# Query product by sevens beside twenty units, with one of its sums made by an accumulating transfer, and another order of the output product

## The chip, the cores and the metric

The kernel runs on one core of one Trainium2 chip. TensorE (PE) multiplies matrices and accumulates in PSUM, VectorE (DVE) adds and multiplies elementwise, ScalarE (ACT) applies functions and casts, GpSimd (POOL) does small odd work and can issue transfers, SyncE (SP) issues transfers only. Each of these engines takes its own instructions in order. The metric is the device time of one execution in microseconds (us); the time given for a kernel is the median of several runs.

## The reference

Two layers run over 256 tokens of width 2048, in float32. Cut to what matters:

```python
for l in range(2):
    h = rms_norm(x, norm1_g[l])
    z = h @ w_in[l]                      # 2048 x 3584: u, v | q | k, v
    z_sgu = gelu(z[..., :2048])          # u and v of the spatial gate, 1024 columns each
    out_a = chunked_sgu(z_sgu, ...)      # u * (causal w_s @ rms_norm(v) + b_s), chunks of 128
    out_b = swa_sink_attention(q, k, v)  # 16 query heads, 4 key heads, window 128, a sink
    mixed = concat(rms_norm(out_a), rms_norm(out_b))
    x = x + mixed @ w_out[l]             # 2048 x 2048
    h2 = rms_norm(x, norm2_g[l])
    x = x + (silu(h2 @ w_gate[l]) * (h2 @ w_up[l])) @ w_down[l]   # inner width 5632
return x
```

## The kernel before

**Products in three passes.** A float32 product is made of three passes in a shorter format: each operand is split into a high part and the rest, and `mm3` (L140 to L142) multiplies high by high, high by rest (`wl`), rest by high. Weights are split as they come: `raw_load` (L97) brings 512 KB, 256 rows by 512 columns, into one of seven buffers `raw`; `split2` has ACT cast it to `wh` (L106, five buffers) and DVE subtract to get `wl` (L107, four buffers). A standard `unit` is one such load and 12 matmuls of 128x512, for the 256 tokens.

**Products by seven.** `seven` computes a 256-row by 2-block product from seven products instead of eight. A weight is seen as blocks b11, b12, b21, b22; the activations have four sums of their blocks, `ext`, made ahead by `extend` (sums `e` on DVE at L265, L268, L271; cast of `ext` on ACT at L275 and subtraction on DVE at L276). For each of four row groups i it loads b11, b12, b22 and runs five `s_unit`s of 6 matmuls: b11, then b11+b12 (sum on DVE, L315), then t2 = b11+b12+b22 (L316), then b22, then b12+b22 (L319). After its use t2 is made into one more sum by a transfer that POOL issues and that adds b21 from memory onto it (L321). After the four groups come four units of b21 and four of the kept t2, between them the closing sums of the banks (`m0` to `m4`, L332 and L336). A product by seven takes 30 steps. Its banks are five PSUM tiles `m`; the standard product beside it takes two others, `dacc`.

**Order.** The program is written as one stream of units. `tick` counts a clock, one for a unit and a half for an `s_unit`; `later(delay, fn)` puts a piece of work at a later count of this clock. The position in the stream decides where a piece stands in the queue of each engine. A scheduler then orders each engine's queue by it.

**Layer 0, its first part.** Eight units of the k and v block (block 4 of `w_in`), then eight each of blocks 2 and 3 (v of the spatial gate). After the first eight (`Q_FROM`), the query product by seven runs beside the remaining `Q_UNITS` = 16 units. The extensions of the activations come at clock `EXT_AT` + half the pair's number after the pair was loaded; x is loaded by rows, at 8 + 3i, and squared for its norm by ACT (L220). `begin` (clock 21) makes the inverse norm; `inv_rms` has DVE make `ms` (L194) and POOL raise it to the power -1/2 (`ir`, L196). `head_inv` squares v, sums per head (`hs`, L238), and after a gap of 2.5 units scales (`scaled` of `v_gate`, L606 and L607). `kv_norm` and `q_norm` do the same for k (L426) and q (L462).

**Attention, gates and the output product.** Six attention units (`attend`, placed by `UNIT_AT`) and four transposes (`END_AT`) run beside the two u blocks of `w_in` and the output product. `spatial` multiplies v by the gate's weights (`ps_g`, L592) into PSUM tiles that `small_ps` takes in turn from three pools; `u_gated` applies the Gelu to u (L620) and transposes it. The output product has a part a (from the spatial gate, four units per column block) and a part b (from attention); `part` adds each to x (L713). `norm_block` transposes the finished column block of x, and makes the activations and their sums for the feed-forward part (`combine`, L282 and L283, and `extend`).

**Feed-forward.** Ten of eleven inner blocks run by seven, 300 steps, beside 104 standard units for the eleventh block and the product with `w_down`. `FF_FIRST` = 3 of the standard units come before the first step; the rest are spread evenly over the steps. In layer 1 the query product by seven runs at the end of layer 0's feed-forward part and beside the first units of layer 1.

Of the kernel before, what the change touches and what calls it, by code (L numbers as in the profile page):

```python
# [20 lines left out]
P = 128  # L21
# [35 lines left out]
SPATIAL_AT = (((6, 9), (6, 9)), ((6, 9), (7, 10)))  # L57
U_AT = (((2, 5), (2, 3)), ((3, 7), (2, 3)))
END_AT = (((23, 27), (31, 33)), ((22, 27), (31, 33)))
FF_FIRST = 3  # L60
EXT_AT = 5
GATE_LOAD = ((14, 23), (5, 15))

# [12 lines left out]
def trunk(ctx, tc, x, xt, w_in, w_q, w_out, w_gate, w_up, w_down, sgu_w, sgu_g, consts,  # L76
# [105 lines left out]
    tab = cp.tile([P, 16], F32, tag="tab", name="tab")  # L182
    nc.scalar.copy(tab, mhalf)
    ident = cp.tile([P, P], F32, tag="ident", name="ident")
# [76 lines left out]

    def extend(g, pool, tag):
# [8 lines left out]
        nc.vector.scalar_tensor_tensor(  # L271
            e[:, 3, :], e[:, 2, :], -1.0, q[:, 2, :], ALU.mult, ALU.subtract
        )
        x = pool.tile([P, 2, 4, P], F32R, tag=tag, name="ext", bufs=8)
        nc.scalar.copy(x[:, 0], e)  # L275
        nc.vector.tensor_tensor(x[:, 1], e, f(x[:, 0]), ALU.subtract)  # L276
        return x

    def combine(ps, lay, col, ext):
        g = gained(ps, lay, col)  # L280
        pair = tp.tile([P, 2, 2, SEQ], F32R, tag="hT", name="hT")
        nc.scalar.copy(pair[:, 0], g)  # L282
        nc.vector.tensor_tensor(pair[:, 1], g, f(pair[:, 0]), ALU.subtract)  # L283
        ext.append(extend(g, ap, "big"))
        return pair

    def seven(src, pairs, ext, out, end=lambda sg: None):
        bank = [pa.tile([P, NB], F32, tag="acc", name=f"m{i}") for i in range(5)]
# [18 lines left out]
        for i in range(4):  # L307
            b11 = raw_load(src(0, 0, i))
            b12 = raw_load(src(0, 1, i))
            b22 = raw_load(src(1, 1, i))  # L310
            t2 = ap.tile([P, 2, NB], F32, tag="spt", name="t2", bufs=4)
            first, last = i == 0, i == 3
            s_unit(b11, 0, i, a_op(0, 0), first, last)
            yield
            nc.vector.tensor_tensor(b11, b11, b12, ALU.add)  # L315
            nc.vector.tensor_tensor(t2, b11, b22, ALU.add)  # L316
            s_unit(b11, 1, i, e_op(1), first, last)
            yield
            nc.vector.tensor_tensor(b12, b12, b22, ALU.add)  # L319
# [35 lines left out]
    def q_product(lay, pairs, ext):  # L355
        q = {"k": 0}
        q["steps"] = seven(
            lambda r, c, i: w_q[lay, c, i, r], pairs, ext, lambda *a: q["out"](*a)
        )
        return q  # L360
# [11 lines left out]
    def first_pair(p, pairs=pairs1, ext=ext1):  # L372
        if p % 2 == 0:
            xrs[0] = ap.tile([P, 4, SEQ], F32, tag="big", name="xr", bufs=8)
        xr = xrs[0][:, 2 * (p % 2) : 2 * (p % 2) + 2, :]
        nc.sync.dma_start(xr, xt[:, 2 * p : 2 * p + 2, :])
        pairs.append(split_gain(xr, 0, C_G1 + 2 * p, "hT"))
        later(EXT_AT + 0.5 * p, lambda: ext.append(extend(gained(xr, 0, C_G1 + 2 * p), tp, "aT")))

# [10 lines left out]
    for i in range(2 * NTOK):  # L390
        later(8 + 3 * i, lambda i=i: load_x(i // 2, i % 2))
    now_q = q_product(0, pairs1, ext1)

    for lay in range(L):
        layer = {}

        def begin(lay=lay, layer=layer, ss1=ss1):
            layer["rstd1"] = finish_rms(ss1, D)
            nsink = small([P, NH], "nsink")
            nc.vector.tensor_scalar(nsink, cst[:, lay, C_SK : C_SK + NH], -1.0, None, ALU.mult)  # L400
            layer["nsink"] = nsink
            nr = small([P, NTOK], "nr")
            layer["nrstd1"] = [nr[:, t : t + 1] for t in range(NTOK)]
            for t in range(NTOK):
                nc.vector.tensor_scalar(
                    layer["nrstd1"][t], layer["rstd1"][t], -1.0, None, ALU.mult
                )

# [3 lines left out]
        def kv_norm(acc, lay=lay, layer=layer, zkv=zkv, kT=kT):  # L412
# [167 lines left out]
        def v_gate(b, acc, lay=lay, layer=layer, gate=gate):  # L580
# [27 lines left out]

            head_inv([v[:, t] for t in range(NTOK)], 8, scaled, 2.5)
            for half in range(2):  # L610
# [55 lines left out]

        later(1 if lay > 0 else 21, begin)
        beside = (pd, "dacc")
# [11 lines left out]
        for i, (gp, t, i0, n) in enumerate(units):  # L680
            at = UNIT_AT[i]
# [34 lines left out]

        early = [part("a", n) for n in range(2)]
        for p in early:
            next(p)
            next(p)  # L720
        for p in early:
            run(p)
        for n in range(2, ND):
            run(part("a", n))
# [281 lines left out]
```

## Time and profile before

| | us |
|---|---|
| median of three runs | 1935.85 (1935.37 to 1936.84) |
| the profiled execution, its own time | 1935.13 |
| its span in the trace | 1933.3 |
| PE busy in the span | 1916.8 |
| DVE busy | 1737.3 |
| ACT busy | 1344.0 |
| POOL busy | 133.5 |

All durations below are of the profiled execution, which lies 0.7 us under the median; some 1.8 us of its time lie outside the span. Matmuls are pipelined: a record of 0.39 us starts 0.227 us after the one before it, so PE's time is read from starts, and a row whose bracket says `[0.73 <-ACT wh L106]` had PE standing 0.73 us until that instruction of ACT ended. The granted clock of TensorE is given for each window: 1.00 is full speed.

### The profile page before, as it was taken

Reading aid. Unit: us, or ns where it says so; the run is one execution under the profiler, and the core shown is the slowest. Engines: PE = TensorE matmul, PEld = TensorE weight load, DVE = VectorE, ACT = ScalarE, POOL = GpSimd, SP = SyncE. Lnnn points to the kernel's source line nnn. Section 1 sums busy time; section 2 is a strip of 40 time slices with the busy share of each in tenths; the row PEclk is TensorE's granted clock in tenths of the full one; section 3 lists DMA queues with packets and bytes.
Section 4 is the critical chain, followed back from the end, with each engine's and each line's share of the span. In section 5 each row is a group of like instructions: output and inputs, shape, how many; then the busy total and the mean of one; then the engine's idle time right before and its main releaser. Section 6 shows DMA issues by size and latency. Waiting matters only on the chain.

```text
span 1933.3 us, 25197 instructions
## 1 busy us (share of the span) xinstructions
PE 1916.8 (99%) x8788; PEld 1570.8 (81%) x8788; DVE 1737.3 (90%) x1870; ACT 1344.0 (70%) x1798; POOL 133.5 (7%) x128
## 2 busy tenths in 40 slices
PE   9999999999999999999999999999999999999999
PEld 6788887888888888888888888878888888888887
DVE  8977679999999999999797766899999999999993
ACT  8667566677676776767777574766776677767774
POOL 0220000000000000000001300000000000000000
PEclk9999999999999999999999999999999999999999
DMA  8865356768677776678567544477678677867773
GB/s 313 250 215 180 133 180 202 227 224 278 209 243 238 247 250 222 230 254 268 189 210 265 176 145 165 163 233 222 227 243 266 223 226 240 275 215 241 240 258 123
DMA packets 120368, 430.62 MB, mean 223 GB/s; under 512 B 13360, under 2 KB 14000, under 8 KB 120240
## 3 DMA queue, kind: packets, MB, share of 16 engines
q1 hardware_dynamic: 105264, 375.52, 52.4%
q0 software_dynamic: 14400, 52.44, 14.8%
q8 instruction: 69, 1.13, 0.2%
q10 hardware_dynamic: 576, 1.05, 0.2%
q14 instruction: 59, 0.48, 0.1%
HBM read 426.85 MB, written 2.10 MB: 222 GB/s over the span
## 4 chain that ended last, share of the span: by engine, by line
PE 93%; DVE 4%; issue 1%; ACT 1%; POOL 1%; DMA 0%; SPq 0%; DVEq 0%; ACTq 0%
PE m L141 14%; PE m L142 14%; PE m L140 14%; PE dacc L140 10%; PE dacc L141 10%; PE dacc L142 10%; PE acc L140 6%; PE acc L141 6%; PE acc L142 6%; DVE wl L107 2%; PE ps_v L545 1%; PE ps_f L213 1%; PE ps_s L496 1%; POOL ir L196 1%; PE ps_t L213 1%
## 5 line engine op out<-in xcount | busy, mean ns | idle before, releaser
L106 ACT CAST wh<-raw 128x1024 fp32r<-128x1024 f32 (+1 forms) x794 | 812.8, 1049 | 391.0 <-DVE raw L315 153.6
L107 DVE TENSOR_TENSOR wl<-raw,wh 128x1024 fp32r<-128x1024 f32 (+1 forms) x794 | 945.3, 1219 | 93.0 <-PE acc L141 33.3
L141 PE MATMUL m<-wl,ext 128*128 128x512 f32 x704 | 277.5, 394 | 5.7 <-DVE wl L107 5.7
L140 PE MATMUL m<-wh,ext 128*128 128x512 f32 x704 | 278.2, 396 | 3.3 <-ACT wh L106 3.0
L142 PE MATMUL m<-wh,ext 128*128 128x512 f32 x704 | 275.4, 391 | 0.0
L140 PE MATMUL dacc<-wh,aT 128*128 128x512 f32 x624 | 243.6, 392 | 0.0
L141 PE MATMUL dacc<-wl,aT 128*128 128x512 f32 x624 | 243.1, 390 | 0.0
L142 PE MATMUL dacc<-wh,aT 128*128 128x512 f32 x624 | 243.0, 390 | 0.0
L107 DVE TENSOR_TENSOR wl<-t,wh 128x1024 fp32r<-128x1024 f32 x176 | 212.2, 1219 | 9.0 <-PE dacc L141 3.5
L106 ACT CAST wh<-t 128x1024 fp32r<-128x1024 f32 x176 | 184.3, 1051 | 46.6 <-DVE t L316 21.6
L140 PE MATMUL m<-wh,hT 128*128 128x512 f32 x528 | 205.9, 390 | 0.0
L141 PE MATMUL m<-wl,hT 128*128 128x512 f32 x528 | 205.5, 389 | 0.0
L142 PE MATMUL m<-wh,hT 128*128 128x512 f32 x528 | 205.5, 389 | 0.0
L141 PEld LDWEIGHTS m<-wl,ext 128*128 128x128 f32 x704 | 132.5, 188 | 38.0 <-DVE wl L107 11.3
L140 PEld LDWEIGHTS m<-wh,ext 128*128 128x128 f32 x704 | 132.4, 188 | 35.3 <-ACT wh L106 8.3
L142 PEld LDWEIGHTS m<-wh,ext 128*128 128x128 f32 x704 | 132.5, 188 | 26.7
L321 POOL DMA_DIRECT2D t<-in_w_gate_dram x80 | 69.7, 871 | 1148.0 <-DVE wl L107 1032.7
L140 PEld LDWEIGHTS dacc<-wh,aT 128*128 128x128 f32 x624 | 117.2, 188 | 25.2 <-ACT dacc L820 1.0
L141 PEld LDWEIGHTS dacc<-wl,aT 128*128 128x128 f32 x624 | 117.2, 188 | 24.4
L142 PEld LDWEIGHTS dacc<-wh,aT 128*128 128x128 f32 x624 | 117.1, 188 | 24.3
L140 PE MATMUL acc<-wh,aT 128*128 128x512 f32 x336 | 134.7, 401 | 0.0
L142 PE MATMUL acc<-wh,aT 128*128 128x512 f32 x336 | 131.4, 391 | 0.0
(148 smaller groups left out, 2796.4 us busy)
## 6 DMA issues: line engine op xcount, KB each, us to landing
raw<-in_w_gate_dram SPq DMA_DIRECT2D x176, 512.0 KB, 5.6
raw<-in_w_up_dram SPq DMA_DIRECT2D x176, 512.0 KB, 5.5
raw<-in_w_down_dram SPq DMA_DIRECT2D x176, 512.0 KB, 4.9
t<-in_w_gate_dram POOLq DMA_DIRECT2D x80, 512.0 KB, 5.8
raw<-in_w_in_dram SPq DMA_DIRECT2D x76, 512.0 KB, 4.8
raw<-in_w_out_dram SPq DMA_DIRECT2D x64, 512.0 KB, 3.2
raw<-in_w_q_dram SPq DMA_DIRECT2D x32, 512.0 KB, 5.0
t<-in_w_q_dram POOLq DMA_DIRECT2D x8, 512.0 KB, 7.2
```

The source lines that it names most:

```text
L106: nc.scalar.copy(wh[:, j : j + step, :], src)
L107: nc.vector.tensor_tensor(wl[:, j : j + step, :], src, f(wh[:, j : j + step, :]), ALU.subtract)
L140: nc.tensor.matmul(acc, ah, wh, start=first, stop=False, skip_group_check=again)
L141: nc.tensor.matmul(acc, ah, wl, start=False, stop=False, skip_group_check=again)
L142: nc.tensor.matmul(acc, al, wh, start=False, stop=last, skip_group_check=again)
L196: anchor[0] = nc.gpsimd.tensor_tensor(r, ms, mhalf[:, :n], ALU.pow)
L213: nc.tensor.transpose(ps[:, j, t * P : (t + 1) * P], blocks[t][:, j * P : (j + 1) * P], ident)
L321: nc.gpsimd.dma_start(t2, src(1, 0, i), accum_op=ALU.add)
L496: nc.tensor.matmul(ps[r][:, i, :], qT[gp][rows, i0 + i, t * P : (t + 1) * P], kT[rows, gp, :nk], start=True, stop=True,)
L545: nc.tensor.matmul(pv[:, r, i], pt[:, (r * n + i) * (t + 1) + b, :], zkv[b][:, cols], start=b == 0, stop=b == t,)
```

## The change

The names of the places shift: L107 becomes L113, L315 L328, L316 L329, L319 L335, L321 L337, L265 to L276 L271 to L284, L196 L202, L592 L615, L606 L629, L620 L643.

- The query product of layer 0 runs beside 20 units: four of the eight units of the first u block (`acc_u`) are taken into `dacc` there. `begin` moves from clock 21 to 18 and the negated norm four units behind it; the k norm, its transposition, and the gap ahead of the v and k scaling in layer 0 (2.5 to 5) move, as do the gate's parts, u's transpositions and the attention's ends by a unit or more.
- In that product the sum b12+b22 is made by a transfer of POOL that adds b22 onto b12 (L331), four transfers in all, in place of four sums on DVE. The feed-forward blocks keep DVE's.
- The split of `ext` comes a unit behind its sums, and the extensions of layer 0 stand at the clock counts of a list, 6.5 to 19.5 in place of 5 to 14.5; x is loaded at 7 + 2.5i.
- In the first row group of each query product and of the first feed-forward block, the `s_unit` of b22 is run second, ahead of the sums.
- `FF_FIRST` is 5 in place of 3.
- The output product runs its parts in the order of a table. Layer 0: a0 and a1 by twos in turn, a2, a3, b0 and b1 by twos in turn, b2, b3. Layer 1: a0 and a1 by twos in turn, b0, b1, a2, b2, a3, b3. Before, in both: a0 and a1 by twos in turn, a2, a3, b0 to b3. A block's norm follows as soon as both its parts are there.
- The first table that ACT loads is that of Gelu.

```diff
-UNIT_AT = (8, 11, 14, 17, 21, 25)
-KV_NORM = (19, 0)
+UNIT_AT = ((8, 11, 14, 17, 20, 24), (8, 11, 14, 17, 21, 25))
+KV_NORM = (20, 0)
+KV_T = (9, 6)
+GAP = (5, 2.5)
-Q_UNITS = (16, 24)
+Q_UNITS = (20, 24)
-FF_FIRST = 3
-EXT_AT = 5
+FF_FIRST = 5
+EXT_AT = (6.5, 7.5, 9.5, 11, 13, 15, 17.5, 19.5)
...
-        x = pool.tile([P, 2, 4, P], F32R, tag=tag, name="ext", bufs=8)
-        nc.scalar.copy(x[:, 0], e)
-        nc.vector.tensor_tensor(x[:, 1], e, f(x[:, 0]), ALU.subtract)
-        return x
+
+        def split():
+            x = pool.tile([P, 2, 4, P], F32R, tag=tag, name="ext", bufs=8)
+            nc.scalar.copy(x[:, 0], e)
+            nc.vector.tensor_tensor(x[:, 1], e, f(x[:, 0]), ALU.subtract)
+            ext.append(x)
+
+        later(1, split)
...
             s_unit(b11, 0, i, a_op(0, 0), first, last)
             yield
+            if soon and first:
+                s_unit(b22, 4, i, e_op(3), first, last)
+                yield
             nc.vector.tensor_tensor(b11, b11, b12, ALU.add)
             nc.vector.tensor_tensor(t2, b11, b22, ALU.add)
+            if s_by_dma:
+                nc.gpsimd.dma_start(b12, src(1, 1, i), accum_op=ALU.add)
             s_unit(b11, 1, i, e_op(1), first, last)
             yield
-            nc.vector.tensor_tensor(b12, b12, b22, ALU.add)
+            if not s_by_dma:
+                nc.vector.tensor_tensor(b12, b12, b22, ALU.add)
             s_unit(t2, 3, i, e_op(2), first, last)
             nc.gpsimd.dma_start(t2, src(1, 0, i), accum_op=ALU.add)
             yield
-            s_unit(b22, 4, i, e_op(3), first, last)
-            yield
+            if not (soon and first):
+                s_unit(b22, 4, i, e_op(3), first, last)
+                yield
             s_unit(b12, 2, i, e_op(0), first, last)
...
-        later(8 + 3 * i, lambda i=i: load_x(i // 2, i % 2))
+        later(7 + 2.5 * i, lambda i=i: load_x(i // 2, i % 2))
...
-                head_inv([z[:, : NKV * HD] for z in zkv], NKV, scaled, 2.5)
-                later(5, to_T)
+                head_inv([z[:, : NKV * HD] for z in zkv], NKV, scaled, GAP[lay])
+                later(KV_T[lay], to_T)
...
-        later(1 if lay > 0 else 21, begin)
+        later(1 if lay > 0 else 18, begin)
...
+        if lay == 0:
+            acc_u = product([w_in[lay, 0, c] for c in range(KT // 2)], pairs1, *beside)
+            for _ in range(Q_UNITS[0] - 16):
+                next(acc_u)
+                with_q()
...
-            u_gated(b, run(block(b)))
+            u_gated(b, run(acc_u if lay == 0 and b == 0 else block(b)))
...
-        early = [part("a", n) for n in range(2)]
...
-        for n in range(ND):
-            run(part("b", n))
-            norm_block(n, ss2, pairs2, lay, C_G2, ext2)
+        parts = {}
+        for name in PARTS[lay].split():
+            kind, n = name[0], int(name[1])
+            if name not in parts:
+                parts[name] = [part(kind, n), 0]
+            next(parts[name][0])
+            parts[name][1] += 1
+            if parts[name][1] == NKV:
+                next(parts[name][0], None)
+                if all(parts.get(f"{k}{n}", (0, 0))[1] == NKV for k in "ab"):
+                    norm_block(n, ss2, pairs2, lay, C_G2, ext2)
...
             return seven(
                 lambda r, c, i: (w_gate, w_up)[c][lay, b, i, r], pairs2, ext2, gated,
-                lambda sg: act_later(b, sg),
+                lambda sg: act_later(b, sg), soon=b == S_BLOCKS[0],
             )
```

How this moves DVE's queue is shown at three places. A row is a line, an operation, output<-inputs and the shape. The first is the second row group of layer 0's query product; `t` is its t2, `raw` a weight, `e` and `ext` an extension. Before:

```order
L265 TENSOR_TENSOR e<-g 128x256
L315 TENSOR_TENSOR raw<-raw 128x1024
L268 SCALAR_TENSOR_TENSOR e<-e,g 128x128
L316 TENSOR_TENSOR t_532<-raw 128x1024
L271 SCALAR_TENSOR_TENSOR e<-e,g 128x128
L319 TENSOR_TENSOR raw<-raw 128x1024
L107 TENSOR_TENSOR wl<-raw,wh 128x1024
L276 TENSOR_TENSOR ext<-e,ext 128x512
L107 TENSOR_TENSOR wl<-t_532,wh 128x1024
```

and now:

```order
L271 TENSOR_TENSOR e<-g 128x256
L328 TENSOR_TENSOR raw<-raw 128x1024
L274 SCALAR_TENSOR_TENSOR e<-e,g 128x128
L113 TENSOR_TENSOR wl<-raw,wh 128x1024
L277 SCALAR_TENSOR_TENSOR e<-e,g 128x128
L329 TENSOR_TENSOR t_540<-raw 128x1024
L113 TENSOR_TENSOR wl<-raw,wh 128x1024
L284 TENSOR_TENSOR ext<-e,ext 128x512
L113 TENSOR_TENSOR wl<-t_540,wh 128x1024
```

The third sum has left DVE, and a split stands in its place. The second place is the scaling of v by the power `ir` of `ms`, in the fourth row group. Before:

```order
L194 TENSOR_SCALAR ms_804<-hs_801 128x16
L107 TENSOR_TENSOR wl<-raw,wh 128x1024
L107 TENSOR_TENSOR wl<-t_814,wh 128x1024
L606 TENSOR_TENSOR v<-v,ir_806 128x512 x2
L607 TENSOR_TENSOR v<-v,gb 128x512 x2
L107 TENSOR_TENSOR wl<-raw,wh 128x1024 x2
```

and now:

```order
L200 TENSOR_SCALAR ms_773<-hs_770 128x16
L113 TENSOR_TENSOR wl<-raw,wh 128x1024 x5
L629 TENSOR_TENSOR v<-v,ir_775 128x512
L328 TENSOR_TENSOR raw<-raw 128x1024
L630 TENSOR_TENSOR v<-v,gb 128x512
L329 TENSOR_TENSOR t_850<-raw 128x1024
L113 TENSOR_TENSOR wl<-raw,wh 128x1024 x2
L629 TENSOR_TENSOR v<-v,ir_775 128x512
```

Between `ms` and the first scaling stand five splits where two stood, and the scaling's parts lie between other work. The third place is the start of layer 0's feed-forward part, its first row group. Before:

```order
L315 TENSOR_TENSOR raw<-raw 128x1024
L316 TENSOR_TENSOR t_2794<-raw 128x1024
L265 TENSOR_TENSOR e<-g 128x256
L319 TENSOR_TENSOR raw<-raw 128x1024
L283 TENSOR_TENSOR hT<-g,hT 128x512
L268 SCALAR_TENSOR_TENSOR e<-e,g 128x128
L107 TENSOR_TENSOR wl<-raw,wh 128x1024
L271 SCALAR_TENSOR_TENSOR e<-e,g 128x128
```

and now:

```order
L328 TENSOR_TENSOR raw<-raw 128x1024
L271 TENSOR_TENSOR e<-g 128x256
L293 TENSOR_TENSOR hT<-g,hT 128x512
L274 SCALAR_TENSOR_TENSOR e<-e,g 128x128
L113 TENSOR_TENSOR wl<-raw,wh 128x1024
L277 SCALAR_TENSOR_TENSOR e<-e,g 128x128
L329 TENSOR_TENSOR t_2830<-raw 128x1024
L271 TENSOR_TENSOR e<-g 128x256
```

The three sums, which stood almost together ahead of the first split, are now spread behind it.

More of the change, by code (lines that the diff above doesn't have):

```diff
@@ L182, in trunk @@
     tab = cp.tile([P, 16], F32, tag="tab", name="tab")
-    nc.scalar.copy(tab, mhalf)
+    nc.scalar.activation(tab, mhalf, AF.Gelu)
     ident = cp.tile([P, P], F32, tag="ident", name="ident")
@@ L260, in gained, with extend @@
         return g
-    def extend(g, pool, tag):
+    def extend(g, pool, tag, ext):
         q = g.rearrange("p j (t c) -> p (j t) c", t=NTOK)
@@ L283, in combine, with seven @@
         nc.vector.tensor_tensor(pair[:, 1], g, f(pair[:, 0]), ALU.subtract)
-        ext.append(extend(g, ap, "big"))
+        extend(g, ap, "big", ext)
         return pair
-    def seven(src, pairs, ext, out, end=lambda sg: None):
+    def seven(src, pairs, ext, out, end=lambda sg: None, soon=False, s_by_dma=False):
         bank = [pa.tile([P, NB], F32, tag="acc", name=f"m{i}") for i in range(5)]
@@ L357, in q_product @@
         q["steps"] = seven(
-            lambda r, c, i: w_q[lay, c, i, r], pairs, ext, lambda *a: q["out"](*a)
+            lambda r, c, i: w_q[lay, c, i, r], pairs, ext, lambda *a: q["out"](*a),
+            soon=True, s_by_dma=lay == 0,
         )
@@ L377, in first_pair @@
         pairs.append(split_gain(xr, 0, C_G1 + 2 * p, "hT"))
-        later(EXT_AT + 0.5 * p, lambda: ext.append(extend(gained(xr, 0, C_G1 + 2 * p), tp, "aT")))
+        at = EXT_AT[p] - clock[0]
+        later(at, lambda: extend(gained(xr, 0, C_G1 + 2 * p), tp, "aT", ext))
     def load_x(t, h, ss=ss1):
@@ L403, in begin, with negate @@
             layer["nrstd1"] = [nr[:, t : t + 1] for t in range(NTOK)]
[L404 to L407, printed above, removed]
+            def negate():
+                for t in range(NTOK):
+                    nc.vector.tensor_scalar(
+                        layer["nrstd1"][t], layer["rstd1"][t], -1.0, None, ALU.mult
+                    )
+            later(4, negate)
         zkv = []
@@ L607, in scaled @@
                     nc.vector.tensor_tensor(v[:, t], v[:, t], gb, ALU.mult)
-            head_inv([v[:, t] for t in range(NTOK)], 8, scaled, 2.5)
+            head_inv([v[:, t] for t in range(NTOK)], 8, scaled, GAP[lay])
             for half in range(2):
```

21 lines of the change are left out of this document (9 added, 12 removed).

## The prediction

> **What bounds the kernel now.** The first view is the page's list of busy times.
>
> ```profile
> PE 1916.8 (99%) x8788; PEld 1570.8 (81%) x8788; DVE 1737.3 (90%) x1870; ACT 1344.0 (70%) x1798; POOL 133.5 (7%) x128
> ```
>
> TensorE's share leaves 16.5 us idle, too coarse to say what can be won. So the second view is the table by windows: length, then busy time of PE, PEld, DVE, ACT, POOL, then granted clock, DMA share, GB/s.
>
> ```profile
> 20.00:40.00 20.00, 20.00 (x90) 16.55 (x89) 18.59 (x29) 17.47 (x32) 0.76 (x1) 1.00 0.88 338
> 40.00:60.00 20.00, 18.13 (x71) 14.04 (x70) 19.48 (x25) 15.29 (x25) 1.15 (x2) 0.91 0.79 225
> 60.00:80.00 20.00, 20.00 (x90) 16.57 (x89) 19.70 (x21) 14.91 (x17) 4.72 (x4) 1.00 0.95 308
> 80.00:100.00 20.00, 17.48 (x71) 14.00 (x70) 15.80 (x23) 10.78 (x14) 8.07 (x4) 0.91 0.75 228
> 300.00:320.00 20.00, 19.32 (x84) 15.33 (x83) 19.93 (x24) 12.73 (x16) 1.81 (x2) 1.00 0.63 177
> 320.00:340.00 20.00, 19.02 (x83) 15.11 (x82) 19.03 (x18) 12.72 (x14) 1.73 (x2) 1.00 0.80 270
> ```
>
> A full window holds 90 matmul records in 20 us, 0.227 us each as the starts also show. Two windows of the layer-0 query stage hold 71: 19 x 0.227 = 4.3 us lost in each. DVE is busy for 19.5 to 19.9 us around three of the four poor windows. The third view is the list of what PE waited for, over the whole run.
>
> ```profile
> PE m L141 <- DVE wl L107: 5.7, 8, 2.5
> PE m L140 <- ACT wh L106: 3.0, 6, 0.7
> ```
>
> `m` are the banks of the product by seven; nearly all waits are there, for a weight's split. The fourth view is the timeline of PE at the places, with the wait in brackets.
>
> ```profile
> 51.11 0.50 PE L140 MATMUL m<-wh,ext 128*128 128x512 f32 x1 [0.73 <-ACT wh L106]
> 52.06 0.49 PE L140 MATMUL m<-wh,ext 128*128 128x512 f32 x1 [0.45 <-ACT wh L106]
> 53.25 0.50 PE L141 MATMUL m<-wl,ext 128*128 128x512 f32 x1 [0.70 <-DVE wl L107]
> ...
> 90.08 0.50 PE L141 MATMUL m<-wl,ext 128*128 128x512 f32 x1 [2.52 <-DVE wl L107]
> ```
>
> The chain of waits between 40 and 60 us tells what stood ahead of that split on DVE, and what came after it; the timelines of ACT, POOL and DVE give the other causes.
>
> ```profile
> 50.65 0.28 DVE e L271
> 50.93 1.14 DVE raw L319
> 52.07 1.14 DVE wl L107
> ...
> 56.71 0.43 PE m L141
> ```
>
> ```profile
> 48.79 0.63 ACT L220 ACTIVATE void<-xres 128x512 bf16<-128x512 f32 x1 [1.95 <-DMA xres<-in_x_dram]
> ```
>
> ```profile
> 81.39 4.97 POOL L196 TENSOR_TENSOR ir<-ms,mhalf 128x16 f32<-128x16 f32 x1 [9.79 <-DVE ms L194]
> ```
>
> ```profile
> 86.39 1.29 DVE L606 TENSOR_TENSOR v<-v,ir 128x512 f32<-128x512 f32 x2 [2.83 <-POOL ir L196]
> ```
>
> The first loss is DVE out of time: extensions (`e`, `ext`) and sums (`raw`, `t`) lie between the splits, and ACT, which must make `wh` first, sat 1.95 us behind a square of x whose load had not landed. The second is DVE standing 2.83 us at the scaling of v, which was queued three splits after its `ms` while the power took 4.97 us. After both, matmuls follow each other every 0.43 us instead of 0.227 for about 3.4 us, which costs some 1.7 us each time: two stalls of 2.5 to 2.7 us in start-to-start excess became losses of 4.3.
>
> The Trainium skill ("TensorE: Matmul & The Clock Gate", What's actually happening) puts the drop to half clock after at least one idle window of about 3.4 us. Here 2.52 us of wait was followed by it, and so were three waits of 0.45 to 0.73 us in 2.6 us. The measurement decides; by the rule taken strictly the half-clock stretches would not belong to these waits, and the sum below would lose 2 x 1.7 us.
>
> **The change, part by part.** Durations that carry the terms, from the groups by shape of the first 100 us (busy, mean ns), and the page's queues:
>
> ```profile
> L107 DVE TENSOR_TENSOR wl<-raw,wh 128x1024 fp32r<-128x1024 f32 x37 | 45.2, 1243 | 2.1 <-ACT wh L106 1.3 <-issue 0.7
> L276 DVE TENSOR_TENSOR ext<-e,ext 128x512 fp32r<-128x512 f32 x8 | 5.4, 686 | 0.0
> L319 DVE TENSOR_TENSOR raw<-raw 128x1024 f32<-128x1024 f32 x4 | 4.9, 1216 | 0.0
> L601 ACT ACTIVATE v<-dacc,ir 128x512 f32<-128x512 f32 x2 | 1.4, 682 | 1.0 <-PE dacc L142 1.0
> L601 ACT ACT_TABLE_LOAD x1 | 1.3, 1283 | 0.0
> ```
>
> ```profile
> q1 hardware_dynamic: 105264, 375.52, 52.4%
> q0 software_dynamic: 14400, 52.44, 14.8%
> ```
>
> ```profile
> DMA to landing us min/median/max: 5.1/6.8/8.3
> ```
>
> The last row is of the four accumulating loads `t<-in_w_q_dram` (L321) between 20 and 110 us. On DVE, back to back, a 128x1024 operation takes 1.14 us (50.93 to 52.07); a standard unit gives PE 12 x 0.227 = 2.72 us for one split, an `s_unit` 1.36.
>
> *Sums and extensions of the query stage.* In the second group the order shows nine DVE instructions, about 7.0 us, for two splits before and for three now: one sum less, one split more. I added up DVE's work in the order of issue by such durations, and PE's work up to the first use of each split. Before, DVE falls behind to -4.3 us at the 21st split and -3.5 to -4 at the 36th to 42nd, which are the two losses. Now it is 5.9 us better at the 21st and 6.4 at the 36th, with at least +1.3 left. This comes from four sums x 1.14 us off DVE, four more standard units (4 x (2.72 - 1.14) us of cover), and extensions begun 1.5 to 5 units later. The x loads go 2.5 units apart; in the order each square now stands 12 us or more behind its load. First loss: 4.3 us gone.
>
> *The v scaling.* Five splits and half of the next group's sums now stand between `ms` and the scaling, 5 x 1.14 = 5.7 us by DVE alone against the power's 4.97 plus hops; the two scalings are also apart. Second loss: 4.3 us gone. In its place the negated scale `nr` now follows its `ms` at once, behind a power on two columns; I take 1.8 us of DVE standing, inside the cover of four ready splits: nothing.
>
> *Accumulating DMAs.* Each issue costs POOL's queue 0.9 us, ahead of the group's own `t` load; behind the first stand the causal mask's load and, for the last, a 5 us power that is over by the time its sum is ready. From the rows of the queues, q0 takes 14.8% / 52.44 against 52.4% / 375.52: twice the engine time per byte, 2.6 us for 512 KB where a load takes 1.3. Four of them add 10.5 us, the four units 5.1 us, to a stage in which the windows of 20 to 100 us use 67 us of 80. Over about 82 us now that is close to full, by share 0.9 to 1.0, and 0.95 was seen with PE at 20.00. The b12 split is needed about 14 us after its sum could be issued; issue and landing take 6.0 to 9.2, so some 5 us are to spare. Ends: nothing, and 4 us with loads late; I take 1.0, nearer the window at 0.95.
>
> The Trainium skill ("SBUF — State Buffer", the trap "DVE blocks DMA") warns that loads issued from GpSimd starve for descriptors while DVE runs two-port operations. The four landings above, with DVE busy over 90%, show no such thing for the additions here; if it held, the lateness rival below would be its price.
>
> *First part of the run.* PE's waits in the first 20 us:
>
> ```profile
> PE acc L141 <- DVE wl L107: 0.7, 1, 0.7
> PE acc L140 <- ACT wh L106: 0.5, 1, 0.5
> ```
>
> Both stand at the fifth to eighth split, where by the sums DVE gains 1.1 to 1.6 us: 1.0 gone. The table load at the start takes the other set: nothing.
>
> *Feed-forward start.* PE in layer 0, and then the waits of layer 1 between 1260 and 1300 us:
>
> ```profile
> 313.63 0.50 PE L140 MATMUL m<-wh,ext 128*128 128x512 f32 x1 [0.68 <-ACT wh L106]
> 337.32 0.50 PE L140 MATMUL m<-wh,ext 128*128 128x512 f32 x1 [0.23 <-ACT wh L106]
> 338.58 0.50 PE L141 MATMUL m<-wl,ext 128*128 128x512 f32 x1 [0.76 <-DVE wl L107]
> ```
>
> ```profile
> PE m L140 <- ACT wh L106: 0.9, 2, 0.7
> PE m L141 <- DVE wl L107: 0.8, 1, 0.8
> ```
>
> With the refill of the array (0.17 to 0.2 each) this is 2.2 us a layer. By the same sums DVE loses 8.1 us on PE through the first groups before, 6.2 now (7.6 and 5.1 in layer 1): two more standard units give 2 x 1.58 us, and the b22 unit comes ahead of the sums. The cover at the start was 8.1 - 2.2 = 5.9, so 0.3 stays in layer 0: 4.1 gone. But two units fewer are left for the 300 steps that follow, 0.2 a block, 0.3 us of cover; late waits such as
>
> ```profile
> 442.24 0.50 PE L141 MATMUL m<-wl,ext 128*128 128x512 f32 x1 [0.31 <-DVE wl L107]
> ```
>
> (two a layer) grow by at most that: 0 to 1.2, I take 0.6.
>
> *Attention.* The four standard units moved to the query stage, and parts of the output product moved, leave the attention of layer 0 with less work around it. Three things follow. One product `ps_g` (L615) stands one matmul behind the last of the first u block and takes over its bank: PE waits for a Gelu out of it, 0.68 us and a hop, I take 0.8 (ends 0.5 and 1.4, both Gelus). One table load more, 1.28 us of ACT, and Exp between the Gelus: ACT has 0 to 1 us of room, I take 0.7. And scaling still waits for powers, as before:
>
> ```profile
> 132.32 0.69 DVE L606 TENSOR_TENSOR v<-v,ir 128x512 f32<-128x512 f32 x1 [2.33 <-POOL ir L196]
> ...
> 136.49 0.69 DVE L462 TENSOR_TENSOR m<-m,ir 128x512 f32<-128x512 f32 x1 [1.57 <-POOL ir L196]
> ```
>
> Now two splits stand behind `ms` ahead of the second v scaling and none ahead of the query scaling, waits of some 2.7 and 3.4 us. PE lost 0.6 there before; I let it stand. The new order of the output product has the same units with the same work; its first norms come earlier, nothing but the feed-forward term.
>
> **Sum.** 4.3 + 4.3 + 1.0 + 4.1 = 13.7 won; 1.0 + 0.6 + 0.8 + 0.7 = 3.1 paid; 10.6 net, off the profiled execution's 1935.13: 1924.5. The median of the runs stands 0.7 above it, so 1925.2.
>
> **The rivals.**
> (1) The larger gain: no payments, the 0.6 goes, and the late feed-forward waits (about 0.8 each, four of them) go as well: 13.7 + 0.6 + 3.1 = 17.4, 1918.4. The unused +1.3 speaks for part of it; that the late waits lie far behind any moved step speaks against.
> (2) Half the gain: loads and accumulations fill the DMA engines in the query stage, and the clock halves again behind the new stalls. 4 us of late loads and two stretches of 1.7 leave 10.6 - 3.0 - 3.4 = 4.2: 1931.6. The share 0.95 between 60 and 80 us speaks for it.
> (3) Slower: accumulations land late. Beyond about 15 us from the sum to the landing, DVE, which takes its queue in order, holds every later split at b12's; four times. To cost more than 10.6 + 3.9 each must take 3.6 us of PE with its half clock (1.9 of wait and 1.7), so a landing of about 17 us, against 8.3 at most in the row. It gives 1940 and more.
> (4) No change: attention in layer 0, where ACT gets switches of tables and the end parts have fewer units before them, loses the gain: six attention units at 1.5 us and two transposes at 1 us are 11 us, about 1936. The chain of waits shows no such wait in either layer now.
> (5) The half-clock stretches have another cause than these waits and stay: 10.6 - 3.4 = 7.2, 1928.6. Three waits of 0.45 to 0.73 us are little for such a drop; that both stretches begin at a wait, within 1 us of its end, speaks against it. This is what the page on the clock gate would give.
>
> **Chances.** The forecast 0.58 and (1), from the same steps, 0.10. Half the gain (2) 0.12, no change (4) 0.06, slower (3) 0.10, (5) 0.04. A measurement of this kernel tells about 0.2%, 3.9 us, from no change; so faster is 0.58 + 0.10 + 0.04 + 0.10 (of (2), the part above 3.9), same 0.02 + 0.06, slower 0.10. The range takes in (1), and the likeliest with its ends (paid 1 to 8), and most of (2): 1917 to 1934; about 0.16 is left above and 0.03 below.
>
> **What would show it.** Right: 90 records in each window of the query stage, clock 1.00 there, no wait of DVE on `ir` at the v scaling near 85 us, b12's accumulations landing within 10 us, no `m` wait over 0.3 us at either feed-forward start, and one PE wait near the end of the first u block. Wrong: DMA as what splits wait for, `wl` or ACT's `wh` waiting for `raw` after an accumulation; half-clock stretches at new places; `aT` waiting for table loads between 140 and 230 us.

## The result, and the profile after

The changed kernel takes 1928.49 us (median of 6 runs) beside 1935.69 us for the kernel before on the same chip: ratio 0.9962, 95% interval 0.995 to 0.9975, 7.2 us faster. The profiled execution's span is 1927.1 us, 6.2 us shorter. The forecast was 10.6 us, 1925.2 us with a range of 1917 to 1934. The kernel before is itself not steady: of its 61 runs beside the experiments, the 35 with a mean clock of 0.998 or less take 1935.8 us in the mean and the 7 with 1.00 take 1933.8, while five of the six runs of the changed kernel have 1.00.

The table by windows, columns as before:

```profile
0.00:20.00 20.00, 17.40 (x63) 11.09 (x64) 14.47 (x30) 15.88 (x30) 0.70 (x6) 1.00 0.88 320
20.00:40.00 20.00, 19.98 (x88) 16.22 (x87) 16.92 (x25) 16.56 (x32) 1.02 (x1) 1.00 1.03 382
40.00:60.00 20.00, 19.07 (x85) 15.34 (x84) 18.85 (x30) 18.89 (x29) 10.89 (x5) 1.00 0.93 283
60.00:80.00 20.00, 19.76 (x87) 15.91 (x86) 17.48 (x20) 12.49 (x17) 13.32 (x5) 1.00 0.90 247
80.00:100.00 20.00, 18.84 (x87) 15.37 (x87) 20.00 (x26) 11.99 (x13) 6.06 (x4) 1.00 1.01 329
120.00:140.00 20.00, 20.00 (x90) 16.29 (x88) 14.96 (x18) 10.89 (x13) 2.90 (x1) 1.00 0.51 176
300.00:320.00 20.00, 20.00 (x89) 16.53 (x89) 19.61 (x18) 13.27 (x14) 1.79 (x2) 1.00 0.81 240
320.00:340.00 20.00, 20.00 (x90) 16.57 (x89) 19.93 (x19) 14.23 (x15) 1.75 (x2) 1.00 0.80 244
```

The two windows with 71 records have 85 and 87, the clock is 1.00 in all, and the feed-forward start is full. Less is left in the query stage, but not nothing; and POOL, busy for 1.15 and 4.72 us in the third and fourth window before, is now busy for 10.89 and 13.32. What PE waited for over the run:

```profile
PE dacc L146 <- ACT wh L112: 1.8, 4, 0.5
PE m L146 <- ACT wh L112: 1.6, 4, 0.6
...
PE m L147 <- DVE wl L113: 1.4, 2, 1.2
PE dacc L147 <- DVE wl L113: 0.9, 1, 0.9
```

The first two lines are new places, in the middle of the feed-forward part:

```profile
396.39 0.50 PE L146 MATMUL m<-wh,ext 128*128 128x512 f32 x1 [0.25 <-ACT wh L112]
397.33 0.73 PE L146 MATMUL dacc<-wh,aT 128*128 128x512 f32 x2 [0.44 <-ACT wh L112]
...
772.58 0.51 PE L146 MATMUL dacc<-wh,aT 128*128 128x512 f32 x1 [0.46 <-ACT wh L112]
```

To compare stages I added up, from the starts of the 128x512 matmuls, what the spacing behind each has over 0.227 us where that is more than 0.1 us (half clock included):

| us lost by PE | first 20 us | 20 to 140 | 140 to 300 | feed-forward, layer 0 | layer 1's first part | feed-forward, layer 1 | sum |
|---|---|---|---|---|---|---|---|
| before | 2.3 | 9.2 | 0.7 | 5.2 | 1.1 | 5.2 | 23.8 |
| after | 1.2 | 3.6 | 0.6 | 4.4 | 1.1 | 4.4 | 15.2 |

8.6 us of losses went, of a span 6.2 us shorter. The other 2.4 us lie in small amounts: the spacings that have less than 0.1 us over 0.227 us take 1.4 us more in sum, the small matmuls 0.6 us more, and the first of the 128x512 matmuls starts 0.25 us later.

### The profile page after: what moved, and what is told of

Same layout as the page of the kernel before. It is cut to its first block, busy times and chain, and to the rows that moved or that the text cites. A ratio compares the mean times of both kernels' runs of the same rounds, so it can differ in the third digit from the quotient of the medians.

```text
span 1927.1 us, 25136 instructions
## 1 busy us (share of the span) xinstructions
PE 1914.2 (99%) x8788; PEld 1568.1 (81%) x8788; DVE 1734.8 (90%) x1866; ACT 1341.1 (70%) x1799; POOL 150.5 (8%) x132
## 3 DMA queue, kind: packets, MB, share of 16 engines
q0 software_dynamic: 14976, 54.53, 15.5%
## 4 chain that ended last, share of the span: by engine, by line
PE 91%; DVE 3%; ACT 2%; issue 2%; DMA 1%; SPq 0%; POOL 0%; ACTq 0%; DVEq 0%; POOLq 0%
PE m L147 13%; PE m L148 13%; PE m L146 13%; PE dacc L146 10%; PE dacc L147 10%; PE dacc L148 10%; PE acc L146 6%; PE acc L147 5%; PE acc L148 5%; DVE wl L113 2%; ACT wh L112 1%; PE ps_v L568 1%; PE ps_f L219 1%; DMA raw<-in_w_in_dram 1%; PE ps_s L519 1%
## 5 line engine op out<-in xcount | busy, mean ns | idle before, releaser
L113 DVE TENSOR_TENSOR wl<-raw,wh 128x1024 fp32r<-128x1024 f32 (+1 forms) x794 | 945.9, 1219 | 85.0 <-PE acc L147 28.5
L113 DVE TENSOR_TENSOR wl<-t,wh 128x1024 fp32r<-128x1024 f32 x176 | 212.3, 1220 | 5.6 <-PE dacc L147 3.0
L337 POOL DMA_DIRECT2D t<-in_w_gate_dram x80 | 69.7, 871 | 1149.7 <-DVE wl L113 1096.5
```

Of the source, the lines that this page charges most:

```text
L113: nc.vector.tensor_tensor(wl[:, j : j + step, :], src, f(wh[:, j : j + step, :]), ALU.subtract)
```

## The experiments

All times are medians beside the kernel before on the same chip; the losses are those of the table's method, from each run's trace. The changed kernel was not run again beside them, so they are set against it by way of the kernel before; where the two ratios' intervals overlap, no difference from the changed kernel is shown.

**The feed-forward start.** Three kernels. The first is the changed kernel with `FF_FIRST = 3`:

```diff
-FF_FIRST = 5
+FF_FIRST = 3
```

> The changed kernel with 3 standard units, not 5, ahead of the first feed-forward step. Theory A (what the two units win at the start is handed back: they shift every later unit against the steps, so that the turn-over of the down product's banks on ScalarE falls on other row groups): waits of up to 2 us a layer come back at the start, the waits near 395, 449, 772 and 834 us and their like in layer 1 go, and the time stays at 1928 to 1930. Theory B (as predicted, the loss of cover is small, 0.6 in all): about 4 us come back and nearly nothing goes, 1932.

Measured: 1926.63 us, ratio 0.9959 (0.9944 to 0.9974). The start's losses are back in layer 0, the ones near 395, 449, 772 and 834 us are gone, and new ones stand at 434 and 508 us: 4.7 us in layer 0 against 4.4, and 3.3 in layer 1 against 4.4. The second is the kernel before with the same number raised to 5, and nothing else:

```diff
-FF_FIRST = 3
+FF_FIRST = 5
```

> The kernel before with 5 standard units, not 3, ahead of the first step, and nothing else. Theory A: the starts near 313 and 337 us lose less, but new waits of 2 to 3 us a layer come between 390 and 840 us, time 1934.5 to 1936.5. Theory B: 3 to 4 us faster, 1932.

Measured: 1935.07 us, ratio 1.0000 (0.9991 to 1.0009). The start is clean (90 records in both windows), and this line of its waits was not there before:

```profile
PE dacc L140 <- ACT wh L106: 1.8, 4, 0.5
```

The losses fall by 0.8 us in each layer: 2.6 and 2.7 us go at the starts, 1.8 and 1.9 us come later. Both runs speak for theory A so far: what is won at the start is mostly handed back. The third keeps 5 units at the start, but puts the later units where 3 would have put them:

```diff
+FF_BASE = 3
...
-            while done < FF_FIRST + (k + 1) * (STD_UNITS - TAIL - FF_FIRST) / HALVES and next(other, False):
+            while done < max(FF_FIRST, FF_BASE + (k + 1) * (STD_UNITS - TAIL - FF_BASE) / HALVES) and next(other, False):
```

> The changed kernel with 5 standard units ahead of the first step, and from the seventh step on the same positions of the standard units as with 3 (two units are pulled ahead, the others stay). Theory A (the shift of the later units against the steps costs): the starts stay without waits, the later waits of a layer fall from about 5 to 2 us, 4 to 6 us faster than the changed kernel, 1923 to 1925. Theory B (two units of cover are missed later): no gain, and new waits within the first block.

Measured: 1928.01 us, ratio 0.9960 (0.9945 to 0.9974). Half of theory A held: the later losses are down to 2.3 us in layer 0 and 2.9 in layer 1, from 4.4 in each. But the start loses again (0.68 us at 305, 1.4 at 329; 2.5 and 2.4 us in the two layers), which makes 4.9 us in layer 0 and 5.3 in layer 1: the two units are missed a few steps later. So it is the shift of all later units that keeps the start clean, and the shift that costs later. It costs small amounts too: the spacings under 0.1 us of excess sum to 16.4 to 16.7 us in the six traces with the places of 5 units and all sums, and to 14.6 to 15.5 in the seven with the places of 3. The place of the units mostly decides where the loss falls, and little how large it is. So I asked what makes the loss:

```diff
...
-            if not s_by_dma:
+            if not s_by_dma and not no_sum:
                 nc.vector.tensor_tensor(b12, b12, b22, ALU.add)
...
-                lambda sg: act_later(b, sg), soon=b == S_BLOCKS[0],
+                lambda sg: act_later(b, sg), soon=b == S_BLOCKS[0], no_sum=True,
```

> The changed kernel without the sum b12+b22 in the feed-forward blocks (80 sums of 1.14 us left out; the output is then not the reference's there). It bounds what VectorE's shortage costs the feed-forward part. If PE's waits there (about 5 us a layer, wherever the standard units stand) come from VectorE: they go, 8 to 9.5 us faster than the changed kernel, 1919 to 1920. If they come from ScalarE's copies at the turn of the down product's banks: 3 us or less faster.

Measured: 1916.53 us in both of two runs, ratio 0.9903 (0.9885 to 0.9921), with 0.3 us lost in each feed-forward part; the small spacings fall by 3.7 us besides, which the expectation did not count. Without 91 us of sums VectorE has room, and ScalarE's copies at the turn of the banks cost no more than what is left. VectorE is the shortage: in 300 us of the changed kernel's feed-forward part it is busy for 295, and without the sums, in the second row, for 282. The edit also spares the cast of b12 its wait for the sum; it does not tell VectorE's time from that wait.

```profile
340.00:640.00 300.00, 298.79 (x1331) 243.90 (x1330) 295.07 (x279) 211.04 (x246) 16.44 (x19) 1.00 0.73 236
```

```profile
340.00:640.00 300.00, 300.00 (x1347) 248.00 (x1346) 282.36 (x264) 214.24 (x249) 16.43 (x19) 1.00 0.77 241
```

**The query stage, part by part.** Each takes one part out of the changed kernel, or does one alone. A warning first: four kernels of this document (3 units ahead, units pulled ahead, sums left out, transfers in the feed-forward part) run this stage by the same instructions in the same order as the changed kernel, and their traces lose 2.2 to 2.7 us between 20 and 140 us where the changed kernel's loses 3.6. So a difference of about 1 us between two traces of this stage is not the work of an edit. The sum on VectorE again:

```diff
-            soon=True, s_by_dma=lay == 0,
+            soon=True,
```

> The changed kernel with the sum b12+b22 on VectorE again, no accumulating transfer for it. If the four sums taken off VectorE carry the query stage's gain: 4 x 1.14 us come back on a VectorE that has 1 to 2 us to spare, stalls between 40 and 100 us grow from 3.5 to 5 to 8 us, with half clock, 1930 to 1933. If the longer cover of 20 units and the spread extensions carry it: 1928 to 1929.

Measured: 1932.32 us, ratio 0.9988 (0.9978 to 0.9997). The stage loses 7.4 us instead of 3.6, with half clock back, in its window from 80 us:

```profile
80.00:100.00 20.00, 17.94 (x71) 14.14 (x70) 17.17 (x21) 10.01 (x11) 8.49 (x4) 0.91 0.69 223
```

The four sums carry 3.8 us of the gain, and more beside the four other traces. The old places of the extensions and x loads:

```diff
-EXT_AT = (6.5, 7.5, 9.5, 11, 13, 15, 17.5, 19.5)
+EXT_AT = (5, 5.5, 7, 8.5, 10, 11.5, 13, 14.5)
...
-        later(7 + 2.5 * i, lambda i=i: load_x(i // 2, i % 2))
+        later(8 + 3 * i, lambda i=i: load_x(i // 2, i % 2))
```

> The changed kernel with the extensions and the x loads of layer 0 at the places of the kernel before. If the spread of the extensions carries part of the query stage's gain: 1 us more in the first 20 us, and VectorE behind again at the second row group, 2 to 4 us between 40 and 60 us, 1930 to 1932. If 20 units and the accumulating transfers suffice: 1928 to 1929.

Measured: 1930.20 us, ratio 0.9973 (0.9963 to 0.9984); 3.8 us lost in the stage, 1.7 in the first 20 us. In the losses the spread is worth 0.5 us in the first 20 us and 0.2 in the stage, less than the first expectation, though the time lies at its edge; beside the four other traces it is 1.1 to 1.6 us in the stage, and the interval overlaps that of the changed kernel. What the spread is worth stays open. The old places move the loss: 0.5 us between 40 and 60 us, 2.9 between 60 and 80. The gap alone, with the gate's product and k's transposition moved behind it, in the kernel before:

```diff
-SPATIAL_AT = (((6, 9), (6, 9)), ((6, 9), (7, 10)))
+SPATIAL_AT = (((9, 12), (8, 11)), ((6, 9), (7, 10)))
...
+KV_T = (9, 5)
+GAP = (5, 2.5)
...
-            head_inv([v[:, t] for t in range(NTOK)], 8, scaled, 2.5)
+            head_inv([v[:, t] for t in range(NTOK)], 8, scaled, GAP[lay])
```

> The kernel before with only the gap ahead of the v and k scaling of layer 0 (5 units, not 2.5), and the spatial product and k's transposition behind it as in the changed kernel. If the wait of VectorE for the power is the whole cause of the second loss: 4.4 us less between 80 and 100 us, the clock 1.00 there, 1931.3. If VectorE is short of time there anyway: the stall shrinks to 1 to 2 us or moves, 1933 or more.

Measured: 1932.28 us, ratio 0.9985 (0.9976 to 0.9995). The second loss is gone whole, the first stands at 4.2 us. That confirms the wait as its whole cause, though in time 2.8 us came and not 4.4: the spans differ by 1.9 us, and the small matmuls of the attention take 2.6 us more (23.9 to 26.5 us, starts of `ps_s` and `ps_p`). The window of the second loss is full, with the clock at 1.00:

```profile
80.00:100.00 20.00, 20.00 (x90) 16.53 (x89) 20.00 (x26) 14.69 (x19) 13.67 (x4) 1.00 0.80 257
```

The power itself took longer than the 4.97 us of before:

```profile
81.68 7.24 POOL L198 TENSOR_TENSOR ir<-ms,mhalf 128x16 f32<-128x16 f32 x1 [9.79 <-DVE ms L196]
```

**What is left in the query stage.** In the changed kernel the chain of the loss near 85 us reads, on POOL, ACT and PE:

```profile
52.16 14.74 POOL L597 TENSOR_SCALAR_AFFINE_SELECT wm<-wm 128x1024 f32<-128x1024 f32 x1 [1.23 <-DMA wm<-in_sgu_w_dram]
...
67.41 1.21 POOL L331 DMA_DIRECT2D raw<-in_w_q_dram  x1
```

```profile
76.43 2.95 ACT L112 CAST wh<-raw 128x1024 fp32r<-128x1024 f32 x3 [3.23 <-DMA raw<-in_w_q_dram]
```

```profile
85.67 0.50 PE L147 MATMUL m<-wl,ext 128*128 128x512 f32 x1 [1.16 <-DVE wl L113]
```

The gate's mask (L597), which took 1.63 us before, holds POOL's queue for 14.74 us; the third accumulating transfer leaves 1.5 us after its sum's input, ACT stands 3.23 us for it, and DVE behind ACT. That is the chain of this one execution. In the four other traces of the same stage the select takes 7.6 to 8.0 us, as in this row of the kernel with 3 units ahead,

```profile
52.53 7.79 POOL L597 TENSOR_SCALAR_AFFINE_SELECT wm<-wm 128x1024 f32<-128x1024 f32 x1 [1.69 <-DMA wm<-in_sgu_w_dram]
```

the third transfer leaves 0.3 us after its input, and nothing is lost near 85 us; 0.6 to 1.1 us are lost near 69 us, where this trace loses 0.5. The mask was moved because of the first trace:

```diff
-GATE_LOAD = ((13, 23), (5, 15))
+GATE_LOAD = ((5, 23), (5, 15))
...
+            if anchor[0] is None:
+                nc.gpsimd.dma_start(wm, sgu_w[lay, :, 8 * b : 8 * b + 8, :])
...
```

> The changed kernel with the first gate's mask (load and select on POOL) eight units earlier, ahead of the second accumulating transfer. If the select that took 14.7 us on POOL between 52 and 67 us, and with it the third transfer that could only be issued behind it, causes the stall of 1.3 us near 84 us: the select takes 1 to 2 us, the third transfer leaves within 0.3 us of its sum's input, that stall goes, 1.0 to 1.5 us faster than the changed kernel. If the transfers are late because the DMA engines are full: the landing stays at 8 to 9 us and the stall stays, and 0.5 MB more to load near 33 us may add 0.5.

Measured: 1930.96 us, ratio 0.9974 (0.9964 to 0.9984), 4.9 us under the kernel before where the changed kernel is 7.2, though the intervals touch. The mask took 1.41 us and nothing is lost near 85 us, but 1.4 us are lost at 71 to 73 us, and the four other traces lose nothing near 85 us without this edit: the first theory is not shown. The load, with nothing to wait for, left at 1.5 us, and the first weight came later (8.94 us for the first product's start, 7.20 in the changed kernel):

```profile
8.94 1.03 PE L146 MATMUL acc<-wh,hT 128*128 128x512 f32 x2 [2.57 <-ACT wh L112]
```

with half clock after it (0.91 in the first 20 us). Next, VectorE's stand behind a power, and what PE misses some units later, in the changed kernel:

```profile
46.94 0.22 DVE L426 TENSOR_SCALAR nr<-ir 128x1 f32<-128x1 f32 x2 [0.83 <-POOL ir L202]
```

```profile
51.15 0.50 PE L147 MATMUL dacc<-wl,hT 128*128 128x512 f32 x1 [0.93 <-DVE wl L113]
```

The negated norm on ScalarE:

```diff
-                    nc.vector.tensor_scalar(
-                        layer["nrstd1"][t], layer["rstd1"][t], -1.0, None, ALU.mult
-                    )
+                    nc.scalar.mul(layer["nrstd1"][t], layer["rstd1"][t], -1.0)
```

> The changed kernel with the negated norm made by ScalarE. If VectorE's stand behind the power at 46 us is what PE misses at 50 us (1.09 us): 0.8 to 1.1 us less there. If VectorE is short by the sums and extensions alone: unchanged, within 0.3.

Measured: 1928.06 us, ratio 0.9958 (0.9941 to 0.9975). At 50 us 0.42 us are lost instead of 1.09 (1.1 in the four other traces too): VectorE's stand behind the power was part of it. In layer 1 the same edit makes ACT late for a transposition:

```profile
PE ps_n L219 <- ACT g L263: 1.0, 1, 1.0
```

The three edits (mask, norm, units pulled ahead) together:

> The three edits together: if they act at separate places, their sum, 6 to 8 us faster than the changed kernel, 1920 to 1923; if the query stage is bound by VectorE or the DMA engines, the first two give nothing together and it is 1923 to 1925.

Measured: 1932.05 us, ratio 0.9983 (0.9974 to 0.9993): their costs added up, not their gains. With the norm's edit in layer 0 alone, the mask's load tied behind the first accumulating transfer, and 3 units ahead:

```diff
...
+                ins = nc.gpsimd.dma_start(b12, src(1, 1, i), accum_op=ALU.add)
+                anchor[0] = anchor[0] or ins
...
```

> The changed kernel with 3 standard units ahead, the negated norm of layer 0 on ScalarE, and the first gate's mask loaded behind the first accumulating transfer, so that it can't leave at the start. If the select near 52 us and the stand of VectorE near 46 us are what is left to win in the query stage: 1.5 to 3 us faster than the changed kernel, 1925 to 1926.5, no wait near 84 us, 0.4 instead of 1.1 near 50 us. If the earlier mask only adds a transfer to full DMA engines: as with 3 units alone or 1 us more, 1926.5 to 1928.

Measured: 1927.43 us, ratio 0.9961 (0.9947 to 0.9974), the second expectation. The mask took 1.29 us and nothing waits near 85 us, but 1.3 us are lost at 69 to 71 instead. No version here is clearly better than the changed kernel; the one with 3 units ahead has the lowest median of those that compute everything, but its ratio, 0.9959, can't be told from 0.9962.

**The accumulating transfer where it has less time.** Since VectorE bounds the feed-forward part, the sum was moved to transfers there too, in two of four row groups (with 3 units ahead):

```diff
...
-                lambda sg: act_later(b, sg), soon=b == S_BLOCKS[0],
+                lambda sg: act_later(b, sg), soon=b == S_BLOCKS[0], s_by_dma=(1, 3),
```

> The changed kernel with 3 standard units ahead, and with the sum b12+b22 made by the accumulating transfer in the second and fourth row group of every feed-forward block too (40 sums of 1.14 us, 46 us of VectorE in all). If VectorE's shortage costs the feed-forward part and a transfer lands within the 8 to 9 us before its split (landing 5.8 us there): most of the 7 to 8 us of waits that the kernel with 3 units still has there go, 1919.5 to 1922. If the transfers land late: VectorE stands for them at the last unit of a group, waits of 1 us and more at many groups, 1926 or slower.

Measured: 1958.27 us, ratio 1.0114 (1.0097 to 1.0131). Each feed-forward part loses 20 us. The landing is no longer than in the query stage; it is too late all the same:

```profile
DMA to landing us min/median/max: 5.5/6.8/8.1
```

Who waited for these transfers between 300 and 960 us, in the view of their line, and what PE waited for:

```profile
  ACT wh L112: 34.8, 16
```

```profile
PE m L147 <- DVE wl L113: 10.2, 19, 0.8
PE ps_f L219 <- DVE aT L778: 5.5, 8, 1.8
```

ACT casts in order, so a late b12 holds every later cast. VectorE is spared some 46 us (40 sums of 1.14), and PE loses 33 us more than in the kernel with 3 units ahead and the sums (46.5 against 14.0).

## Why the prediction was right or wrong

The direction, the order of size and the main mechanisms were right; the size was 10.6 us where 7.2 came. The terms that were too large are those of the query stage and of the feed-forward start. Of the signs named for being right, the clock, the scaling of v, the landings and the two starts came as said; 85 to 88 records stood where 90 were named, and ACT's wait for an accumulated `raw`, a sign of being wrong, was seen. By the steps:

- *The two losses of the query stage, 8.6 us, less 1.0 for the transfers:* 5.6 us came (9.2 to 3.6, the 0.6 near 138 us among it). DVE no longer waits for `ir` at the v scaling, and no half clock is left. The terms "first loss: gone" and "nothing" for the negated norm failed by 1.1 us: the running sum left too little cover for a stand of VectorE at 46 us (0.83 us, about half of the 1.8 allowed for it). The step on the transfers failed in its spare time: b12 was said to be needed 14 us after its sum could be issued. The view of ACT shows the cast, which runs ahead of the split, ready for it 7.3 us after the sum's input in the third group (65.9 to 73.2 us). Landings of 5.4 to 8.9 us were as forecast. The DMA share, forecast at 0.9 to 1.0, was 0.90 to 1.03 in the windows of 20 to 100 us; by the rows of the queues an accumulation of 512 KB takes 2.9 us of the engines and a load 1.4, not 2.6 and 1.3. That POOL's select could hold the transfers behind it was not in the sum.
- *The rival of late transfers* was right as a mechanism and too mild in its price: it needs no landing of 17 us. Where b12 follows sooner, landings of 6.8 us cost 33 us more than the sums did. In the query stage it cost 1.3 us at 85 us in the changed kernel's trace, and nothing there in the four others.
- *First 20 us, 1.0:* 1.2 came; but kernels that differ only later range from 0.5 to 2.4 there, so this is no clean test.
- *Feed-forward start, 4.1, less 0.6:* 1.6 us of losses went, and in the kernel before the same edit alone changed the time by nothing that could be measured. The 4.1 came, and more: the two starts lost 5.3 us by the table's method and now lose nothing. The failing step is "But two units fewer are left for the 300 steps that follow, 0.2 a block, 0.3 us of cover", and the 0.6 taken for it: the later losses rose by 3.7 us in the two layers, and the small spacings by the 1.4 us named above. The step counted the two blocks that waited before, while any of ten blocks may come to wait on an engine that is busy 98% of the time. Two units moved ahead do not give VectorE any time; 80 sums left out did.
- *Attention, 0.8 and 0.7 to pay, and 0.6 left near 138 us:* nothing came of the two payments as waits, and the 0.6 went too. `ps_g` follows its matmul 0.35 us later with no wait, so the wait for a Gelu that I had put there did not come; the reason stays open. DVE stands 3.0 us for a power twice, until 133 and 149 us, where 2.7 and 3.4 were forecast, and PE misses nothing.
- *Half clock:* that the stretches belong to the waits is borne out, since they went with them. Rival (5) gave 1928.6 us, 0.1 from what was measured, but its condition is not met: the clock is 1.00 in every window shown. That its number fits is chance. Yet the size of the waits is not all that decides. In the kernel before with 5 units, three waits of the same size at 50 us were followed by no half clock (78 records, 1.00), and the first loss was 2.7 us instead of 4.2. The clock's records in the traces show why. Within a trace every change of the clock lies a whole multiple of 3.413 us from the others (before: down at 53.66 us, up at 57.07, down at 91.20). Counted in such stretches, from the first change to 1.00 up to the last matmul, the 14 traces have eight in which PE stood 1.86 us or more, and after each the clock was halved; it was halved after none with 1.81 us or less. In the kernel before the three waits fall into one stretch, and PE is busy for 1.54 us of it:

```profile
50.24:53.65 3.41, 1.54 (x5) 0.72 (x5) 3.41 (x5) 3.41 (x5) 0.00 (x0) 1.00 0.54 208
53.66:57.07 3.41, 3.41 (x10) 2.64 (x9) 3.41 (x4) 2.76 (x3) 0.89 (x1) 0.50 0.46 154
```

  With 5 units a border at 51.79 us parts them, 1.06 us before it and 0.80 behind it:

```profile
48.38:51.79 3.41, 2.35 (x10) 1.38 (x8) 3.41 (x5) 3.10 (x6) 0.00 (x0) 1.00 0.95 355
51.79:55.20 3.41, 2.60 (x10) 1.95 (x11) 3.41 (x5) 3.41 (x6) 0.00 (x0) 1.00 0.36 105
```

  So some 1.5 us of the first loss were a matter of where the waits fell between these borders. The Trainium skill ("TensorE: Matmul & The Clock Gate", What's actually happening) calls the gate's window free-running, which agrees; its idle of a whole window of about 3.4 us preceded none of the drops shown here.

## What to carry to other kernels

Where an engine is busy for 98% of a long part, moving work ahead of that part moves the loss and does not lessen it; ask what takes work off that engine. A transfer that replaces a sum has to land before the first reader in any queue, and that is the engine that runs ahead (here the cast), not the one that used to add. A load that is moved earlier without anything to wait for goes to the front of the queue, where it may cost more than it saves.

## What the runs showed of the hardware that was not expected

POOL's select of 128x1024 took 1.1 us where VectorE stood still (at 63 us, with the old spread), and 5 to 15.6 us in some runs where VectorE added and subtracted without a pause. In the changed kernel VectorE's rows leave no gap between 52.16 and 65.94 us; the first is 0.03 us long, the select ends 0.9 us behind it, and the VectorE instruction over its end takes 2.00 us where its like takes 1.22:

```profile
64.72 1.22 DVE L328 TENSOR_TENSOR raw<-raw 128x1024 f32<-128x1024 f32 x1
65.97 2.00 DVE L329 TENSOR_TENSOR t<-raw 128x1024 f32<-128x1024 f32 x1
```

In two other runs (5.09 and 15.6 us) it was the same: a gap of 0.03 to 0.04 us, an end 0.9 to 1.0 us later, an instruction of 2.00 us. It is not always POOL that is held: in the kernel before, the select at 69 us took 1.63 us under gapless splits, and the split over its end took 2.11 us. The power on 128x16 shows it more mildly: 2.90 us with VectorE idle, 7.24 us without a gap, but 3.87 us without a gap in the kernel with 3 units ahead. In the kernel before the power of 4.97 us ended 2.8 us after VectorE stopped (83.56 to 86.36), nearly the time it takes alone. So the wait behind the second loss was probably in part of VectorE's own making; what decides which of the two is held, no run here shows. The Trainium skill ("SBUF — State Buffer", Who interferes with whom) says that a VectorE instruction with two SBUF inputs shares a read port with GpSimd's reads and that one blocks the other for a whole instruction; the traces agree, and add that the blocked one can wait through more than ten instructions. The prediction looked only at descriptors, and for these the traces showed no such thing.
